# A decoder trunk on one core: another place for the compression MLP's first products in the second layer, and a written-out order for the mixers' preparation buffers

## The chip, the cores and the metric

One core of one Trainium2 chip runs the whole program in one launch. The metric is the device time of one execution in microseconds (us), as the median of several executions.

## What is computed

A decoder of DEPTH = 2 layers on one sequence of S = 256 tokens and D = 1024 channels, all in float32. Cut to what matters here:

```
for l in range(DEPTH):
    h = rms_norm(x, norm1_g[l]);  proj = h @ w_in[l]
    ya = dsa_mixer(...)      # A, number 0: sparse attention with an indexer
    yb = moba_mixer(...)     # B, number 1: block attention
    yc = nsa_mixer(...)      # C, number 2: compressed + selected + window attention
    yd = swa_mixer(...)      # D, number 3: sliding window, 2 kv heads
    x = x + sum_n(sigmoid(gate_n) * (y_n @ w_branch[n])) @ w_out[l]
    x = x + conv_ffn(rms_norm(x, norm2_g[l]))
# inside nsa_mixer, for keys (i = 0) and values (i = 1): 15 blocks of 32 tokens
c_i = gelu((blocks_i + pe_i) @ w1_i) @ w2_i     # w1_i: 2048 x 128
```

The product with `w1_i` is the first product of the compression MLP. It can run as soon as the mixer C has written the blocks with their position encoding, and the mixer C needs it for its compressed keys and values, thus for everything that comes after them.

## The kernel before

**Weights.** All weights are streamed from HBM by SyncE's queue into three buffers `raw` of 1 MB, in the order of a list `plan`, filled by `rows_chunk` and walked by `next(it)`. A chunk of a big matrix holds 4 blocks of 128 rows by 512 columns and is cut in two pieces. Each piece is split in two fp32r parts: ScalarE copies the high part (tile `hi`, `split_hi`), VectorE subtracts it and keeps the rest (tile `lo`, `split_lo`); there are four buffers of each. TensorE then runs `macs`: for each piece 8 matmuls with `hi` (against the activations' high and low parts, `ahi` and `alo`) and 4 with `lo` (against `ahi`). Half a gate (512 of its 1024 columns) is two chunks, so four pieces or 48 matmuls; half a branch's output product is one piece or 12.

**Order of the work.** `Flow` is a planner that runs while the program is built. Streams (Python generators) yield the engine that they want next, the futures that they need and the rings from which they take a buffer; `Flow.run` keeps a model clock for each engine, starts the stream that its clocks let start first, and breaks ties by priority. The instructions of each engine are in the order in which the planner gave them out, and every engine executes its own strictly in that order. The main stream (`main`) goes through the columns of `w_in` for the four mixers, then through a list written out by hand, `SEQ`:

```
SEQ = [("gate", 0, 0), ("gate", 0, 1), ("hidden", 0, 0), ("hidden", 1, 0), ("gate", 1, 0),
       ("gate", 1, 1), ("branch", 0, 0), ("branch", 0, 1), ("gate", 2, 0), ("gate", 2, 1),
       ("branch", 1, 0), ("branch", 1, 1), ("gate", 3, 0), ("branch", 2, 0), ("branch", 2, 1),
       ("branch", 3, 0), ("gate", 3, 1), ("branch", 3, 1)]
```

Both the list of chunks (so the loads on SyncE) and TensorE's work follow it: `gate_of(n, half)`, `hidden(i, ch, hid)`, `branch_out(n, half)`. After it come `w_out`, the convolutional FFN and, in the first layer, the second layer's start.

**The mixers** (`dsa`, `moba`, `nsa`, `swa`) run beside that list: VectorE, ScalarE and GpSimd prepare queries and keys (per-head RMS with a power of -1/2 on GpSimd, rotary), and their transposes (tile `tr`), scores and products with the values stand on TensorE in between the gates' matmuls. All four use one set of preparation buffers `rt`, `qr`, `kr`, `kn` (ring `prep_r`, one entry), so the preparation of one mixer starts only when the one before has given the set back: `(prep,) = yield "ACT", [pf, tab_f[l]], [prep_r]`. Which mixer gets it next is the planner's choice.

**hidden(i, ch, hid)** is the first product of the compression MLP: 16 slices of `w1_i` (raw, not split) against `kr`, which holds C's blocks with the position encoding added (`kr<-kn,col`, the step of `nsa` after which it sets `hid.ready`). TensorE cannot pass it: where `kr` is late, everything behind it waits. The halves' sums `hsum` (`hidden_sum`) lead on to the compressed attention (`nsa_cmp`) and to the two `attend2` streams of C, the last products of which (`tr<-f,slotQ`) close C's output in `slotQ`. `y_T` splits that output for `branch(2,0)` into `yhi` (ScalarE) and `ylo` (VectorE).

A row of the profile calls nearly every instruction L214, the line of the helper in `Eng` that issues it, and L242 for loads; so instructions are told apart by their tiles. Each of the transposes is a matmul that writes `tr`; `mm` and `sc` are the other PSUM banks. Of the two layers, the first has its `hidden` at 101.92 us of the span, the second at 524.06 us.

Of the kernel before, what the change touches and what calls it, by code (L numbers as in the profile page):

```python
# [231 lines left out]
def trunk(ctx: ExitStack, tc: tile.TileContext, a, out):  # L232
# [15 lines left out]
    def ring(n, shape, name, dt=F32):  # L248
# [12 lines left out]
    prep_r = Ring([(sb([128, NT, 512], "rt"), sb([128, NT, 256], "qr"), sb([128, NT, 256], "kr"),  # L261
                    sb([128, NT, 256], "kn"))])
# [73 lines left out]
    col_f = [Fut() for _ in range(DEPTH)]  # L336
    tab_f = [Fut() for _ in range(DEPTH)]
# [46 lines left out]
    def rows_chunk(src, k0, k1, c0, c1):  # L384
# [7 lines left out]
        if not plan:  # L392
# [1 line left out]
        plan.append(Chunk(ap, (nk, n), cut))  # L394


    SEQ = [("gate", 0, 0), ("gate", 0, 1), ("hidden", 0, 0), ("hidden", 1, 0), ("gate", 1, 0),
           ("gate", 1, 1), ("branch", 0, 0), ("branch", 0, 1), ("gate", 2, 0), ("gate", 2, 1),
           ("branch", 1, 0), ("branch", 1, 1), ("gate", 3, 0), ("branch", 2, 0), ("branch", 2, 1),
           ("branch", 3, 0), ("gate", 3, 1), ("branch", 3, 1)]  # L400
    FIRST, LAST = [n for op, n, _ in SEQ if op == "branch"][0], SEQ[-1][1]
    PRIO = (4, 19, 7, 6)
    PORDER = (0, 2, 1, 3)
    CH_A, CH_C = [(0, 384), (384, 680)], [(1448, 1832), (1832, 2100)]
# [4 lines left out]
    for l in range(DEPTH):  # L409
        wi = a["w_in"][l]  # L410
        for kg in range(2):
            for _, c0, c1 in COLS[:2]:
                rows_chunk(wi, 4 * kg, 4 * kg + 4, c0, c1)
        for _, c0, c1 in COLS[2:]:
            for kg in range(2):
                rows_chunk(wi, 4 * kg, 4 * kg + 4, c0, c1)
        for op, n, half in SEQ:
            if op == "gate":
                for kg in range(2):
                    c0 = 2612 + n * D + half * 512  # L420
                    rows_chunk(wi, 4 * kg, 4 * kg + 4, c0, c0 + 512)
            elif op == "hidden":
                ap = a["c_cmp_w1"][l, n].rearrange("(c p) h -> p c h", p=128)
                plan.append(Chunk(ap, (16, 128), []))
            elif n == LAST:
                rows_chunk(a["w_branch"][l, n], 0, 2, half * 512, half * 512 + 512)
            elif half == 0:
                ap = a["w_branch"][l, n].rearrange("(k p) n -> p k n", p=128)
                plan.append(Chunk(ap, (2, D), [lambda v, h=h: v[:, :, h * 512:h * 512 + 512] for h in range(2)]))
        for kg in range(2):  # L430
            for half in range(2):
                rows_chunk(a["w_out"][l], 4 * kg, 4 * kg + 4, half * 512, half * 512 + 512)
        up = a["w_up"][l].rearrange("(k p) (g n) -> p k g n", p=128, g=2)
        for c in range(0, KF, 2):
            for g in range(2):
                plan.append(Chunk(up[:, :, g, c * 128:c * 128 + 256], (8, 256),
                                  [lambda v, h=h: v[:, :, h * 128:h * 128 + 128] for h in range(2)]))
        for half in range(2):
            for k0, k1 in DOWN:
                rows_chunk(a["w_down"][l], k0, k1, half * 512, half * 512 + 512)  # L440
# [358 lines left out]

    def dsa(l, pa, pf, y, yf):  # L800
        m = M[l]
        (prep,) = yield "ACT", [pf, col_f[l]], [prep_r]
        rt, qr, kr, kn = prep
        latT = kn[:, :, 128:256]
        tl = yield from head_rstd(pa[:, :, None, 256:384], 1, 128, sm1["rl"], rt, [])
        tb, = yield "PE", [], [tr_r]
        tp = tb[:, :256].rearrange("p (t q) -> p t q", t=NT)
        for t in range(NT):
            te = P.transpose(tp[:, t, :], pa[:, t, 256:384], ident)
        yield "ACT", [te], []  # L810
        te = A.activation(latT, tp, AF.Copy, scale=m["col"][:, 16:17])
        tr_r.give(tb, te)
        tb, = yield "PE", [te], [tr_r]
        kvp = tb[:, :256].rearrange("p (t q) -> p t q", t=NT)
        for t in range(NT):
            te = P.matmul(kvp[:, t, :], latT[:, t, :], m["kvup"], start=True, stop=True)
        ti = yield from head_rstd(pa[:, :, None, 640:672], 1, 32, sm1["ri"], rt, [])
        yield "DVE", [te, tl], []
        tkv = V.tensor_tensor(kvA, kvp, sm1["rl"][:, :, None].to_broadcast([128, NT, 128]), op=ALU.mult)
        tr_r.give(tb, tkv)  # L820
        yield "DVE", [tab_f[l]], []
        tq = yield from rope(qr.rearrange("p t (h u d) -> p t h u d", u=1, d=32), heads(pa[:, :, 384:640], 32), 8, 32,
                             cosi, sini, rt, [])
        (ix,) = yield "PE", [], [qk_r]
        iqT, ikT = ix[:, 0:512].rearrange("p (k s) -> p k s", k=2), ix[:, 512:768].rearrange("p (k s) -> p k s", k=1)
        tq = yield from T_pairs(iqT, qr, 2, [tq])
        yield "DVE", [ti], []
        ikn = kn[:, :, None, 0:32]
        tn = V.tensor_tensor(ikn, pa[:, :, None, 640:672], sm1["ri"][:, :, None, None].to_broadcast([128, NT, 1, 32]), op=ALU.mult)
        krd = kr[:, :, 0:128]  # L830
        tk = yield from rope(krd.rearrange("p t (h u d) -> p t h u d", h=1, d=32), ikn, 1, 32, ci, si, rt, [tn], dup=4)
        tk = yield from T_pairs(ikT, krd, 1, [tk])
        iw = th(sm1["iw"], 8)
        yield "DVE", [], []
        V.tensor_scalar(iw, pa[:, :, 672:680], 1.0 / 16.0, None, op0=ALU.mult)
        idx_d = []
        idx_f = Fut()
        fin = qk_done(ix, idx_d, idx_f, NT)
        self_f = [Fut() for _ in range(NT)]
        for t in range(NT):  # L840
            fl.spawn(indexer(t, iqT, ikT, iw, [tq, tk], fin, self_f[t]), 5 + t)
        trk = yield from head_rstd(kvA[:, :, None, 0:64], 1, DH, sm1["rk"], rt, [tkv])
        yield "DVE", [trk], []
        knv = kn[:, :, None, 0:64]
        tn = V.tensor_tensor(knv, kvA[:, :, None, 0:64], sm1["rk"][:, :, None, None].to_broadcast([128, NT, 1, 64]), op=ALU.mult)
        tk = yield from rope(krd.rearrange("p t (h u d) -> p t h u d", h=1, d=64), knv, 1, DH, cc[:, 1], ss_[:, 1], rt, [tn], dup=2)
        trq = yield from head_rstd(heads(pa[:, :, 0:256]), H, DH, sm1["rqA"], rt, [])
        yield from scaled(sm1["sA"], sm1["rqA"], H, trq)
        tq = yield from rope(qr.rearrange("p t (h u d) -> p t h u d", u=1, d=64), heads(pa[:, :, 0:256]), H, DH,
                             cc[:, 0], ss_[:, 0], rt, [])  # L850
        (qk,) = yield "PE", [], [qk_r]
        qT, kT = qk[:, 0:512].rearrange("p (k s) -> p k s", k=2), qk[:, 512:768].rearrange("p (k s) -> p k s", k=1)
        tq = yield from T_pairs(qT, qr, 2, [tq])
        tk = yield from T_pairs(kT, krd, 1, [tk])
        prep_r.give(prep, tk)
        fin = qk_done(qk, [], yf, 1)
        fl.spawn(attend2(10, qT, lambda h: 0, kT, lambda h, b: kvA[:, b, 64:128], th(sm1["sA"], H), sel,
                        y, [tq, tk] + self_f, fin=fin), 10)
# [35 lines left out]
        f.t = V.tensor_tensor(sel[t], sel[t], mask, op=ALU.min)  # L894

    def moba(l, pb, pf, y, yf):
        (prep,) = yield "ACT", [pf, tab_f[l]], [prep_r]
        rt, qr, kr, kn = prep
        tr = yield from head_rstd(heads(pb[:, :, 0:512]), 8, DH, sm1["rB"], rt, [])
        yield from scaled(sm1["sB"], sm1["rB"], 8, tr)  # L900
# [13 lines left out]
                        th(sm1["sB"], H), [tri[:, 128:], tri], y, [tq, tk], fin=fin), 20)  # L914

    def swa(l, pd, pf, y, yf):
        (prep,) = yield "ACT", [pf, tab_f[l]], [prep_r]
        rt, qr, kr, kn = prep
        tr = yield from head_rstd(heads(pd[:, :, 0:384]), 6, DH, sm1["rD"], rt, [])
        yield from scaled(sm1["sD"], sm1["rD"], 6, tr)  # L920
# [16 lines left out]

    def nsa(l, pc, pf, y, yf, hid):
        m = M[l]
        (prep,) = yield "DVE", [pf, tab_f[l]], [prep_r]  # L940
        rt, qr, kr, kn = prep
        kvd = kr.rearrange("p t (i u d) -> p t i u d", i=2, u=2)
        t1 = yield from rope(kvd[:, :, 0:1], pc[:, :, None, 256:320], 1, DH, cosd, sind, rt, [], dup=2)
# [322 lines left out]
    def main():  # L1266
# [13 lines left out]
        for l in range(DEPTH):  # L1280
# [11 lines left out]
            proj = (pa, pb, pc, pd)  # L1292
            ys = [p[:, :, 0:256] for p in proj]
            yf = [Fut() for _ in range(4)]
            def mixer(n, f):
                if n == 2:
                    fl.spawn(nsa(l, pc, f, ys[2], yf[2], hid), PRIO[2])
                else:
                    fl.spawn((dsa, moba, None, swa)[n](l, proj[n], f, ys[n], yf[n]), PRIO[n])
# [3 lines left out]
            for i, kg in [(0, 0), (1, 0), (0, 1), (1, 1)] + [(i, kg) for i in range(2, len(COLS)) for kg in range(2)]:  # L1303
                n, c0, c1 = COLS[i]
# [4 lines left out]
                if kg == 1:  # L1309
                    f = Fut()  # L1310
# [54 lines left out]
                        k0 = 4 * half + 2 * j  # L1365
                        fl.spawn(rows_T(mg[:, :, 128 * k0:128 * k0 + 256], [f], mT, k0, mf[2 * half + j], scale=0.5), 2)

            order = [n for op, n, half in SEQ if op == "branch" and half == 0]
            for i, n in enumerate(order):
                yTs[n] = [], Fut()  # L1370
                fl.spawn(y_T(ys[n], yf[n], *yTs[n]), 2)
            for op, n, half in SEQ:
                if op == "gate":
                    yield from gate_of(n, half)
                elif op == "hidden":
                    yield from hidden(n, next(it), hid)
                else:
                    yield from branch_out(n, half)
# [108 lines left out]
```

## Time and profile before

| | |
|---|---|
| median of 3 runs | 851.69 us (851.65 to 853.23) |
| the profiled execution's own time | 850.18 us |
| its span in the trace | 848.4 us |
| mean granted TensorE clock | 0.994 of full speed |
| TensorE busy with matmuls | 835.4 us (98%) |
| VectorE / ScalarE / GpSimd busy | 673.0 (79%) / 543.8 (64%) / 36.5 us (4%) |
| moved by DMA | 149.91 MB, mean 177 GB/s |

Times inside the trace are us from the start of the span. "PE" is TensorE's matmuls, "DVE" VectorE, "ACT" ScalarE, "POOL" GpSimd, "SP" SyncE. Idle time in front of an instruction is given with what released it. The granted clock (PEclk) is a share of full speed: 1.00 is 2.4 GHz, 0.50 is 1.2 GHz, a value in between a stretch with both.

### The profile page before, as it was taken

To read this page: it belongs to the slowest core of one execution; us is meant where nothing else is said; L and a number is where in the kernel's file an instruction comes from. 1 tells how busy PE (TensorE), PEld (TensorE's weight loads), DVE (VectorE), ACT (ScalarE), POOL (GpSimd) and SP (SyncE) were. 2 spreads that over 40 slices of the span, in tenths; PEclk is the share of its full clock that TensorE was granted. 3 is DMA by queue.
4 is the path that set the end of the run, shared out by engine and by line. 5 is a ranking of instruction groups with operands and counts; after the bars stand their busy time and mean duration, and the time that the engine had idled before them with its cause. 6 is when DMAs were issued, how large, how long until landed. Compare 5 with 4: busy or idle time off the path is not lost.

```text
span 848.4 us, 14190 instructions
## 1 busy us (share of the span) xinstructions
PE 835.4 (98%) x5459; PEld 733.1 (86%) x5459; DVE 673.0 (79%) x1327; ACT 543.8 (64%) x941; POOL 36.5 (4%) x33
## 2 busy tenths in 40 slices
PE   9999999999999999999999997999999999999998
PEld 8987787888899999978898875878878999999886
DVE  5799989788579999975458989977676799999552
ACT  6673775765478888844366667766445788888431
POOL 0111111000000000000001110100000000000000
PEclk9999999999999999999999997999999999999999
DMA  7754563444647666546456453435455465665550
GB/s 264 248 199 149 178 216 106 159 162 153 219 138 229 207 201 197 186 153 210 132 168 211 157 173 115 148 117 182 162 192 192 149 199 199 200 199 199 175 197 26
DMA packets 103414, 149.91 MB, mean 177 GB/s; under 512 B 4072, under 2 KB 62258, under 8 KB 103346
## 3 DMA queue, kind: packets, MB, share of 16 engines
q1 hardware_dynamic: 103346, 149.00, 52.6%
q8 instruction: 43, 0.70, 0.3%
q14 instruction: 25, 0.20, 0.1%
HBM read 147.94 MB, written 1.05 MB: 176 GB/s over the span
## 4 chain that ended last, share of the span: by engine, by line
PE 86%; DVE 7%; DMA 2%; POOL 2%; ACT 1%; issue 1%; SPq 0%; DVEq 0%; ACTq 0%
PE mm L214 75%; PE tr L214 6%; PE sc L214 5%; DVE lo L214 2%; DMA raw<-in_w_in_dram 1%; POOL rB L214 1%; DVE acc L214 1%; DVE rt L214 1%; DMA x<-in_x_dram 1%; POOL rD L214 1%; DVE m L214 1%; DVE f L214 1%; ACT f L214 0%; ACT hi L214 0%; SPq L242 0%
## 5 line engine op out<-in xcount | busy, mean ns | idle before, releaser
L214 DVE TENSOR_TENSOR lo<-raw,hi 128x1024 fp32r<-128x1024 f32 (+2 forms) x280 | 328.7, 1179 | 99.4 <-ACT hi L214 95.3
L214 ACT ACTIVATE hi<-raw 128x1024 fp32r<-128x1024 f32 (+2 forms) x280 | 283.0, 1022 | 152.6 <-PE mm L214 132.4
L214 PE MATMUL mm<-hi,ahi 128*128 128x512 f32 (+4 forms) x480 | 176.0, 372 | 0.6 <-ACT hi L214 0.6
L214 PE MATMUL mm<-hi,alo 128*128 128x512 f32 (+4 forms) x480 | 172.2, 364 | 0.0
L214 PE MATMUL mm<-ahi,hi 128*128 128x256 f32 x640 | 149.9, 276 | 0.0
L214 PE MATMUL mm<-alo,hi 128*128 128x256 f32 x640 | 149.7, 276 | 0.0
L214 PEld LDWEIGHTS mm<-alo,hi 128*128 128x128 f32 x640 | 120.1, 188 | 0.1
L214 PEld LDWEIGHTS mm<-ahi,hi 128*128 128x128 f32 x640 | 120.2, 188 | 0.1
L214 PE MATMUL mm<-lo,ahi 128*128 128x512 f32 (+4 forms) x480 | 118.2, 369 | 0.0
L214 PEld LDWEIGHTS mm<-hi,ahi 128*128 128x128 f32 x480 | 90.2, 188 | 15.2 <-issue 1.7
L214 PEld LDWEIGHTS mm<-hi,alo 128*128 128x128 f32 x480 | 90.3, 188 | 12.0
L214 PEld LDWEIGHTS mm<-lo,ahi 128*128 128x128 f32 x480 | 83.0, 188 | 13.2 <-issue 1.3
L214 PE MATMUL mm<-hi,slotQ 128*128 128x512 f32 x352 | 89.6, 395 | 0.0
L214 PE MATMUL mm<-ahi,lo 128*128 128x256 f32 x640 | 86.9, 276 | 0.0
L214 PEld LDWEIGHTS mm<-hi,slotQ 128*128 128x128 f32 x352 | 66.1, 188 | 15.4
L214 PEld LDWEIGHTS mm<-ahi,lo 128*128 128x128 f32 x640 | 79.1, 188 | 0.0
L214 ACT ACTIVATE f<-f,col 128x256 f32<-128x256 f32 x88 | 48.1, 594 | 6.4 <-DVE f L214 6.4
L214 PE MATMUL mm<-lo,slotQ 128*128 128x512 f32 x176 | 48.7, 396 | 0.0
L214 PEld LDWEIGHTS mm<-lo,slotQ 128*128 128x128 f32 x176 | 33.0, 188 | 7.6
L214 ACT ACTIVATE qk<-f,col 128x256 f32<-128x256 f32 x88 | 39.2, 495 | 0.0
L214 ACT ACTIVATE f<-f,nmx 128x128 f32<-128x128 f32 (+1 forms) x80 | 35.3, 444 | 4.7 <-DVE nmx L214 4.7
L214 DVE SCALAR_TENSOR_TENSOR f<-f,col,f 128x254 f32<-128x254 f32 x88 | 38.2, 478 | 0.0
(235 smaller groups left out, 1038.6 us busy)
## 6 DMA issues: line engine op xcount, KB each, us to landing
raw<-in_w_up_dram SPq DMA_DIRECT2D x44, 1024.0 KB, 5.0
raw<-in_w_in_dram SPq DMA_DIRECT2D x40, 1024.0 KB, 4.8
raw<-in_w_down_dram SPq DMA_DIRECT2D x20, 1024.0 KB, 4.9
raw<-in_w_out_dram SPq DMA_DIRECT2D x8, 1024.0 KB, 5.3
raw<-in_w_branch_dram SPq DMA_DIRECT2D x6, 1024.0 KB
raw<-in_w_in_dram SPq DMA_DIRECT2D x7, 768.0 KB
raw<-in_w_in_dram SPq DMA_DIRECT2D x4, 592.0 KB, 3.7
raw<-in_w_in_dram SPq DMA_DIRECT2D x4, 536.0 KB, 5.7
```

The lines of the kernel that those rows point to most:

```text
L214: fn(*a, **k)
```

## The change

Three edits. `SEQ` becomes a list per layer, `SEQS`; the first layer's is the old one, and in the second layer's `("gate", 1, 0)` stands ahead of the two `hidden`, so that 48 matmuls and two loads of 1 MB come before them and not behind. A mixer's request for the preparation buffers also waits for its turn, in a fixed order per layer: A, B, C, D in the first, A, B, D, C in the second. And `nsa` asks for the buffers as a step of ScalarE, not VectorE, as the other three do (that concerns the planner's choice alone; no instruction belongs to the request).

```diff
--- before.py
+++ after.py
@@ -394,11 +394,15 @@
         plan.append(Chunk(ap, (nk, n), cut))
 
 
-    SEQ = [("gate", 0, 0), ("gate", 0, 1), ("hidden", 0, 0), ("hidden", 1, 0), ("gate", 1, 0),
+    SEQS = [[("gate", 0, 0), ("gate", 0, 1), ("hidden", 0, 0), ("hidden", 1, 0), ("gate", 1, 0),
            ("gate", 1, 1), ("branch", 0, 0), ("branch", 0, 1), ("gate", 2, 0), ("gate", 2, 1),
            ("branch", 1, 0), ("branch", 1, 1), ("gate", 3, 0), ("branch", 2, 0), ("branch", 2, 1),
-           ("branch", 3, 0), ("gate", 3, 1), ("branch", 3, 1)]
-    FIRST, LAST = [n for op, n, _ in SEQ if op == "branch"][0], SEQ[-1][1]
+           ("branch", 3, 0), ("gate", 3, 1), ("branch", 3, 1)],
+            [("gate", 0, 0), ("gate", 0, 1), ("gate", 1, 0), ("hidden", 0, 0), ("hidden", 1, 0),
+           ("gate", 1, 1), ("branch", 0, 0), ("branch", 0, 1), ("gate", 2, 0), ("gate", 2, 1),
+           ("branch", 1, 0), ("branch", 1, 1), ("gate", 3, 0), ("branch", 2, 0), ("branch", 2, 1),
+           ("branch", 3, 0), ("gate", 3, 1), ("branch", 3, 1)]]
+    FIRST, LAST = [n for op, n, _ in SEQS[0] if op == "branch"][0], SEQS[0][-1][1]
     PRIO = (4, 19, 7, 6)
     PORDER = (0, 2, 1, 3)
     CH_A, CH_C = [(0, 384), (384, 680)], [(1448, 1832), (1832, 2100)]
@@ -414,7 +418,7 @@
         for _, c0, c1 in COLS[2:]:
             for kg in range(2):
                 rows_chunk(wi, 4 * kg, 4 * kg + 4, c0, c1)
-        for op, n, half in SEQ:
+        for op, n, half in SEQS[l]:
             if op == "gate":
                 for kg in range(2):
                     c0 = 2612 + n * D + half * 512
@@ -799,7 +803,8 @@
 
     def dsa(l, pa, pf, y, yf):
         m = M[l]
-        (prep,) = yield "ACT", [pf, col_f[l]], [prep_r]
+        (prep,) = yield "ACT", [pf[0], pf[1], col_f[l]], [prep_r]
+        pf[2]()
         rt, qr, kr, kn = prep
         latT = kn[:, :, 128:256]
         tl = yield from head_rstd(pa[:, :, None, 256:384], 1, 128, sm1["rl"], rt, [])
@@ -894,7 +899,8 @@
         f.t = V.tensor_tensor(sel[t], sel[t], mask, op=ALU.min)
 
     def moba(l, pb, pf, y, yf):
-        (prep,) = yield "ACT", [pf, tab_f[l]], [prep_r]
+        (prep,) = yield "ACT", [pf[0], pf[1], tab_f[l]], [prep_r]
+        pf[2]()
         rt, qr, kr, kn = prep
         tr = yield from head_rstd(heads(pb[:, :, 0:512]), 8, DH, sm1["rB"], rt, [])
         yield from scaled(sm1["sB"], sm1["rB"], 8, tr)
@@ -914,7 +920,8 @@
                         th(sm1["sB"], H), [tri[:, 128:], tri], y, [tq, tk], fin=fin), 20)
 
     def swa(l, pd, pf, y, yf):
-        (prep,) = yield "ACT", [pf, tab_f[l]], [prep_r]
+        (prep,) = yield "ACT", [pf[0], pf[1], tab_f[l]], [prep_r]
+        pf[2]()
         rt, qr, kr, kn = prep
         tr = yield from head_rstd(heads(pd[:, :, 0:384]), 6, DH, sm1["rD"], rt, [])
         yield from scaled(sm1["sD"], sm1["rD"], 6, tr)
@@ -937,7 +944,8 @@
 
     def nsa(l, pc, pf, y, yf, hid):
         m = M[l]
-        (prep,) = yield "DVE", [pf, tab_f[l]], [prep_r]
+        (prep,) = yield "ACT", [pf[0], pf[1], tab_f[l]], [prep_r]
+        pf[2]()
         rt, qr, kr, kn = prep
         kvd = kr.rearrange("p t (i u d) -> p t i u d", i=2, u=2)
         t1 = yield from rope(kvd[:, :, 0:1], pc[:, :, None, 256:320], 1, DH, cosd, sind, rt, [], dup=2)
@@ -1292,7 +1300,17 @@
             proj = (pa, pb, pc, pd)
             ys = [p[:, :, 0:256] for p in proj]
             yf = [Fut() for _ in range(4)]
+            order_of = ((0, 1, 2, 3), (0, 1, 3, 2))[l]
+            turn = dict((n, Fut()) for n in order_of)
+            turn[order_of[0]].t = 0.0
+
+            def next_turn(n):
+                i = order_of.index(n) + 1
+                if i < 4:
+                    turn[order_of[i]].t = 0.0
+
             def mixer(n, f):
+                f = [f, turn[n], lambda: next_turn(n)]
                 if n == 2:
                     fl.spawn(nsa(l, pc, f, ys[2], yf[2], hid), PRIO[2])
                 else:
@@ -1365,11 +1383,11 @@
                         k0 = 4 * half + 2 * j
                         fl.spawn(rows_T(mg[:, :, 128 * k0:128 * k0 + 256], [f], mT, k0, mf[2 * half + j], scale=0.5), 2)
 
-            order = [n for op, n, half in SEQ if op == "branch" and half == 0]
+            order = [n for op, n, half in SEQS[l] if op == "branch" and half == 0]
             for i, n in enumerate(order):
                 yTs[n] = [], Fut()
                 fl.spawn(y_T(ys[n], yf[n], *yTs[n]), 2)
-            for op, n, half in SEQ:
+            for op, n, half in SEQS[l]:
                 if op == "gate":
                     yield from gate_of(n, half)
                 elif op == "hidden":
```

The GpSimd steps of the preparation show the order of the mixers: B, C, D in the first layer (`rB`, `rC`, `rD`) and B, D, C in the second (`rB`, `rD`, `rC`), before and after the change alike. In the first layer TensorE's instructions stand in the same order as before. In the second they part behind the last matmuls of `gate(0,1)`.

**TensorE, second layer, from the last matmul of `gate(0,1)`.** Before (`raw_73,kr` and `raw_71,kr` are the two `hidden`, `hi_76` the first piece of `gate(1,0)`):

```order
L214 MATMUL mm_64<-lo_79,ahi 128x512
L214 MATMUL tr_70<-cst,kr 128x128 x4
L214 MATMUL tr_69<-cst,kr 128x128 x4
L214 MATMUL tr_70<-cst,f_0_82 128x128 x4
L214 MATMUL mm_65<-raw_73,kr 15x128 x16
L214 MATMUL mm_66<-raw_71,kr 15x128 x16
L214 MATMUL tr_69<-cst,f_1_83 128x128 x4
L214 MATMUL tr_70<-cst,f_1_83 128x128 x4
L214 MATMUL mm_63<-hi_76,ahi 128x512
```

The change, from the end of the second piece of `gate(1,0)` (`lo_81`) into its third (`hi_74`):

```order
L214 MATMUL mm_65<-lo_81,ahi 128x512
L214 MATMUL mm_66<-lo_81,ahi 128x512
L214 MATMUL mm_65<-hi_74,ahi 128x512
L214 MATMUL mm_65<-hi_74,alo 128x512
L214 MATMUL mm_66<-hi_74,ahi 128x512
L214 MATMUL mm_66<-hi_74,alo 128x512
L214 MATMUL tr_69<-cst,kr 128x128 x4
L214 MATMUL tr_70<-cst,f_0_82 128x128 x4
L214 MATMUL mm_65<-hi_74,ahi 128x512
```

and from its last matmul:

```order
L214 MATMUL mm_66<-lo_79,ahi 128x512
L214 MATMUL mm_63<-raw_72,kr 15x128 x16
L214 MATMUL tr_70<-cst,f_1_83 128x128 x4
L214 MATMUL tr_69<-cst,f_1_83 128x128 x4
L214 MATMUL mm_64<-raw_73,kr 15x128 x16
L214 MATMUL tr_70<-cst,hsum 128x15
L214 MATMUL tr_69<-f_3_85,slotQ 64x128 x4
L214 MATMUL tr_69<-f_2_84,slotQ 64x128 x8
```

The `hidden` products, which stood ahead of all of `gate(1,0)`, are now behind its 48 matmuls. The transposes of `kr`, which stood ahead of it too, are now within it: the first group (D's keys) four matmuls into the second piece, the second group (C's blocks), which is shown, four matmuls into the third.

**TensorE, second layer, the last products of C with its values** (`f_2_84`, `f_3_85` with `slotQ`). Before, with the first matmuls of the piece that follows:

```order
L214 MATMUL tr_69<-f_2_84,slotQ 64x128 x4
L214 MATMUL tr_69<-f_3_85,slotQ 64x128 x8
L214 MATMUL mm_65<-hi_76,ahi 128x512
L214 MATMUL mm_65<-hi_76,alo 128x512
L214 MATMUL mm_66<-hi_76,ahi 128x512
L214 MATMUL mm_66<-hi_76,alo 128x512
```

The change:

```order
L214 MATMUL tr_69<-f_2_84,slotQ 64x128 x4
L214 MATMUL tr_69<-f_3_85,slotQ 64x128 x8
L214 MATMUL mm_65<-lo_79,ahi 128x512
L214 MATMUL mm_66<-lo_79,ahi 128x512
L214 MATMUL mm_65<-lo_79,ahi 128x512
L214 MATMUL mm_66<-lo_79,ahi 128x512
L214 MATMUL mm_63<-hi_76,yhi_114 128x512
L214 MATMUL mm_63<-hi_76,ylo_115 128x512
L214 MATMUL mm_64<-hi_76,yhi_114 128x512
L214 MATMUL mm_64<-hi_76,ylo_115 128x512
```

Before, they stood in `gate(2,1)`, and 96 more matmuls of gates and branches came between them and `branch(2,0)`, whose first is `sc_68<-hi_76,yhi_114`; now they stand within `gate(3,0)`, four matmuls with `lo_79` ahead of `branch(2,0)`, whose first is `mm_63<-hi_76,yhi_114`.

**VectorE, second layer, at D's norm** (`rD` from the sum of squares to the scale `sD`; the power of -1/2 on GpSimd stands between `rD<-rD` and `sD<-rD`). Before:

```order
L214 COPY qk_88<-tr_69 128x512
L214 TENSOR_TENSOR lo_79<-raw_72,hi_75 128x1024
L214 TENSOR_REDUCE rD<-rt 128x12
L214 RECIPROCAL rd_113<-den_111 128x4
L214 TENSOR_SCALAR rD<-rD 128x12
L214 TENSOR_SCALAR f_1_83<-f_1_83,rd_113 128x256 x2
L214 TENSOR_SCALAR sD<-rD 128x8
```

The change:

```order
L214 COPY qk_88<-tr_69 128x512
L214 TENSOR_TENSOR lo_79<-raw_72,hi_75 128x1024
L214 RECIPROCAL rd_113<-den_111 128x4
L214 TENSOR_TENSOR lo_80<-raw_73,hi_76 128x1024
L214 TENSOR_REDUCE rD<-rt 128x12
L214 TENSOR_SCALAR f_1_83<-f_1_83,rd_113 128x256
L214 TENSOR_SCALAR rD<-rD 128x12
L214 TENSOR_TENSOR lo_81<-raw_73,hi_77 128x1024
L214 COPY f_2_84<-tr_69 128x512
L214 TENSOR_TENSOR lo_78<-raw_71,hi_74 128x1024
L214 TENSOR_SCALAR sD<-rD 128x8
```

Between the reduction and `sD` VectorE now has two splits (`lo_81`, `lo_78`) and a copy, where before it had two scalings; one split (`lo_80`) also stands ahead of the reduction.

On SyncE, the two chunks of `gate(1,0)` are now loaded ahead of the two of `w1`, the other way round than before.

## Rows read from the trace of the kernel before

**Rows 1.** Windows by stage: us, busy of PE, PEld, DVE, ACT, POOL, PEclk, DMA.

```profile
440.00:515.23 75.23, 75.03 (x462) 63.72 (x460) 67.23 (x181) 47.55 (x83) 11.06 (x6) 1.00 0.53 175
515.23:528.39 13.16, 7.36 (x84) 5.66 (x85) 11.89 (x42) 9.82 (x29) 1.64 (x1) 0.61 0.32 108
528.39:614.75 86.36, 86.36 (x503) 69.65 (x502) 67.11 (x184) 51.95 (x112) 2.21 (x2) 1.00 0.45 156
```

**Rows 2.** Waits of PE in the whole span: total us, times, longest.

```profile
PE tr L214 <- DVE kr L214: 3.0, 1, 3.0
PE tr L214 <- DVE den L214: 1.8, 1, 1.8
PE mm L214 <- DVE kr L214: 1.0, 1, 1.0
...
PE sc L214 <- DVE slotP L214: 0.2, 1, 0.2
```

**Rows 3.** Chain of waits in 514 to 530: start us, us, what.

```profile
517.45 0.62 DVE kr L214 x3
...
520.46 0.49 DVE kr L214 x2
```

**Rows 4.** Windows of the idle and the half-speed pieces of 515.23 to 528.39.

```profile
515.23:518.21 2.98, 0.00 (x1) 0.03 (x1) 2.98 (x13) 1.07 (x2) 0.00 (x0) 0.83 0.69 226
518.21:519.31 1.10, 1.08 (x4) 0.68 (x4) 0.66 (x5) 0.53 (x3) 0.00 (x0) 0.50 0.90 349
519.31:521.10 1.79, 0.00 (x0) 0.03 (x1) 1.70 (x7) 1.79 (x10) 0.00 (x0) 0.50 0.00 0
521.10:523.04 1.94, 1.94 (x8) 1.54 (x8) 1.43 (x5) 1.89 (x8) 0.00 (x0) 0.50 0.00 0
...
524.06:527.61 3.55, 3.55 (x65) 2.59 (x66) 3.39 (x13) 3.40 (x7) 1.64 (x1) 0.53 0.13 31
```

**Rows 5.** Windows at full clock: the first layer's hidden, and eight transposes.

```profile
101.92:103.79 1.87, 1.87 (x65) 1.66 (x64) 1.86 (x11) 1.47 (x4) 0.00 (x0) 1.00 0.78 300
507.79:508.58 0.79, 0.79 (x9) 0.79 (x8) 0.00 (x0) 0.15 (x1) 0.79 (x1) 1.00 1.03 399
```

**Rows 6.** DVE in order of time: start us, us, what [idle before].

```profile
504.39 1.23 DVE L214 TENSOR_TENSOR lo<-raw,hi 128x1024 fp32r<-128x1024 f32 x1
505.53 0.95 DVE L214 TENSOR_REDUCE rD<-rt 128x12 f32<-128x768 f32 x1
...
509.11 0.17 DVE L214 TENSOR_SCALAR sD<-rD 128x8 f32<-128x8 f32 x1 [1.90 <-POOL rD L214]
...
511.73 1.22 DVE L214 TENSOR_TENSOR lo<-raw,hi 128x1024 fp32r<-128x1024 f32 x1
...
523.65 1.16 DVE L214 TENSOR_TENSOR kr<-kn,col 128x120 f32<-128x120 f32 x4
```

**Rows 7.** POOL, the power step of D (first and second layer), and DVE beside it.

```profile
131.03 1.22 DVE L214 TENSOR_TENSOR lo<-raw,hi 128x1024 fp32r<-128x1024 f32 x1
...
131.20 3.17 POOL L214 TENSOR_TENSOR rD<-rD,mhalf 128x12 f32<-128x12 f32 x1 [9.22 <-DVE rD L214]
...
506.77 2.31 POOL L214 TENSOR_TENSOR rD<-rD,mhalf 128x12 f32<-128x12 f32 x1 [18.28 <-DVE rD L214]
```

**Rows 8.** PE, DVE and ACT in order of time, from C's last products to branch(2,0).

```profile
592.80 0.68 DVE L214 TENSOR_TENSOR slotQ<-slotQ,tr 128x512 f32<-128x512 f32 x1
...
603.78 0.64 ACT L214 ACTIVATE yhi<-slotQ 128x512 fp32r<-128x512 f32 x1 [2.65 <-DVE mg L214]
...
604.45 0.69 DVE L214 TENSOR_TENSOR ylo<-slotQ,yhi 128x512 fp32r<-128x512 f32 x1
...
613.65 1.08 PE L214 MATMUL mm<-lo,ahi 128*128 128x512 f32 x4
614.57 0.39 PE L214 MATMUL sc<-hi,yhi 128*128 128x512 f32 x1
```

**Rows 9.** DMA issues (page, part 6): count, KB each, us to landing.

```profile
raw<-in_w_in_dram SPq DMA_DIRECT2D x40, 1024.0 KB, 4.8
```

## The prediction

> **What bounds the kernel.** TensorE is busy 98% of the span, so the time is its matmuls plus what it waits or runs slowly. I read four views in turn. The waits of PE [rows 2] are short but for three, 3.0, 1.8 and 1.0 us, all for VectorE. The windows by stage [rows 1] put them together: from 515.23 to 528.39 PE is busy 7.36 of 13.16 us at a mean clock of 0.61, whereas it is busy 75.03 of 75.23 us in the stage before and all of the 86.36 us behind, at 1.00. The chain of waits [rows 3] says who is late: VectorE's steps to `kr`, for D's keys (ready 517.45 + 0.62 = 518.07), then C's blocks (520.95), then the blocks with their encoding, which `hidden` needs. The pieces of that stretch [rows 4] show the second half of the loss: after 2.98 us without a matmul the clock is at half, and stays there nearly to the end of `hidden`.
>
> **What the change can give back.** Three idle pieces: 2.98, 1.79 and 524.06 - 523.04 = 1.02, together 5.79 us [rows 4]. The work between them runs at half speed, and its price at full speed stands elsewhere [rows 5]: eight transposes take 0.79 us, so four 0.40, and the first layer's `hidden` takes 1.87 us. So 1.10 - 0.40 = 0.70, 1.94 - 0.79 = 1.15 and 3.55 - 1.87 = 1.68, together 3.53 us. In all **9.32 us**, if TensorE now has 48 matmuls of `gate(1,0)` to do while VectorE finishes `kr`, and if `kr` is not late again.
>
> **Is kr in time?** Four matmuls of 128x512 take 614.57 - 613.65 = 0.92 us [rows 8], a piece of twelve 2.75 us. From 515.23 PE comes to D's transposes at 515.23 + 2.75 + 0.92 = 518.9, to C's at 515.23 + 5.5 + 0.92 + 0.4 = 522.05, and to `hidden` at 515.23 + 11.0 + 1.2 for the twelve transposes = 527.4. VectorE's side is replayed from rows 6 in the changed order; operations overlap by some 0.08 us, so a split counts 505.53 - 504.39 = 1.14 us. At 505.53 come a reciprocal (0.1), the split now ahead (1.14), the reduction (0.87), a scaling (0.3) and `rD` (0.1): 508.05. Then GpSimd's power: 2.31 us in the second layer, where VectorE idled until `sD`, 3.17 us in the first, where a split ran beside it, so 0.86 more for a split [rows 6, 7]. Now two splits and a copy stand beside it (1.14 + 0.6 + 1.14 = 2.9, until 510.95). So `sD` comes between 511.0 (no slowing) and 513.3 (the power only after both splits, 510.95 + 2.31); by the nearest row, two splits at 0.86, at 508.05 + 0.1 + 2.31 + 1.72 = 512.2, which I take. Before it came at 509.11.
>
> From `sD` to D's `kr` there were 518.07 - 509.11 = 8.96 us, in which stood two splits, the one at 511.73 and another [rows 6]. Both now stand elsewhere: 8.96 - 2.28 = 6.7, so 518.9 and 0.1 of hand-over, 0.1 behind PE. C's `kr` took 2.9 us more; one split (1.14) and a scaling (0.2) now stand among that, and 0.46 us of waiting for slow transposes falls away: 522.7, some 0.5 behind a PE that is itself 0.1 late. `hidden`'s `kr` took from `sD` 523.65 + 1.16 - 509.11 = 15.7 us; less two splits, plus one, 14.55: 526.75, **0.7 us ahead of PE** at 527.4, 1.3 with the waits before it. So of the three waits some 0.6 us is left.
>
> A rule of the Trainium skill speaks against this step. "SBUF — State Buffer", section "SBUF: two separate sides", makes the port pair that VectorE and GpSimd share an exclusive lock: a VectorE operation with two SBUF inputs, or a GpSimd one, holds it for the whole instruction and the other fully blocks. By the Trainium skill the copy would let the power in and the second split would wait for it, or the power would wait for both, which puts `sD` up to 1.1 us later than my sum. The 3.17 against 2.31 us agrees with a lock; that VectorE is held up in turn no row here shows. By the rule's worst order the time would be that of rival 1, 845.3.
>
> **What the change adds.** C's compressed attention begins 3.3 us later (527.4 for 524.06), and TensorE reaches everything behind sooner. The order shows what is late next: C's last products with its values now stand four matmuls ahead of `branch(2,0)`. Before, `slotQ` was finished at 593.48 and `branch(2,0)` began at 614.57, 21 us later [rows 8], so no wait there is seen. Now the closing addition (0.61), `yhi` (0.62) and `ylo` (0.60), durations of rows 8, stand between, and three hand-overs of about 0.05; 2.0 us, less the 0.92 of the four matmuls: a **wait of 1.0 us**. Bounds: 0, if TensorE is late itself and covers it; 2.1, if a split of 1.14 stands in VectorE's way. I take 1.0 as the sum of the rows.
>
> Other waits: the 0.6 us above, bounds 0 (`sD` at 511.0) and 1.7 (513.3). VectorE was busy 67.23 + 11.89 + 67.11 = 146.2 of 174.75 us from 440 to 614.75 [rows 1]; without 9.3 us it is busy 88%, and `gate(3,0)` now writes the PSUM banks that `branch(1,0)` left 12 matmuls (2.75 us) earlier, with four operations of VectorE of some 0.6 us between. For that I take one wait like the nearest row, 0.2 us [rows 2], bounds 0 and 1. Together **0.8**.
>
> At nothing I cost: the exchange of loads (a chunk lands 4.8 us after its issue [rows 9]; the chunk of `gate(1,0)` now takes the buffer that `w1` had, over 10 us before it is needed, and `w1` comes while `gate(1,0)` runs; if this cover went, `hidden` would wait up to 4.8 us); the written-out turns, as GpSimd's order of B, C, D and B, D, C shows that the planner had chosen the same; and the request on ScalarE, which has no instruction. The first layer's order on TensorE is unchanged. Below zero, a gain besides the 9.32 us, I exclude: elsewhere PE has no idle time beyond 0.2 us in 161 us [rows 1].
>
> **Sum**, against the profiled execution: 850.18 - 9.32 + 1.0 + 0.8 = 842.66 us. The median stands 851.69 - 850.18 = 1.51 higher, so **844.2 us**. The bounds of the added terms come to 0 and 2.1 + 1.7 + 1.0 = 4.8, so this case lies between 842.4 and 847.2.
>
> **Rivals.**
> 1. *`kr` late again.* The power waits for both splits, `sD` comes at 513.3: 1.1 us more of waits at the transposes, too short to bring the clock down: 845.3. For it: 3.17 beside one split. Against: even so the chain meets 48 matmuls, 11 us, where it was 5.8 us late. 0.10.
> 2. *The half speed is no part of the gain.* The three runs lie 1.5 us above the profiled one, so something differs between executions; if the clock did not fall in them, only 5.79 - 1.8 = 3.99 us is gained: 847.7. Against: 2.98 us without a matmul brought it down here [rows 4]. 0.10.
> 3. *A new wait brings the clock down again.* If the wait at `branch(2,0)` or one on C's chain grows to 2 or 2.5 us in one piece, it may bring back the half speed, as 2.98 us did [rows 4], with 3.53 us as bound: 850.18 - 9.32 + 2.25 + 3.53 + 0.8 + 1.51 = 849.0. For it: VectorE at 88%. 0.12.
> 4. *Slower.* C's output gets so late that PE stands at `branch(2,0)` for w and then runs slowly: w + 3.53 + 0.8 outweighs 9.32 from w = 5.0 us on. With w = 8 it is 850.18 - 9.32 + 8 + 3.53 + 0.8 + 1.51 = 854.7. C's chain took 593.48 - 524.06 = 69.4 us; PE comes to `branch(2,0)` at 614.57 - 9.32 + 0.8 = 606.0, so from `hidden` at 528 the chain to `slotQ` would have to take 606.0 + 5.0 - 1.2 - 528 = 82 us. Against: it would have to stretch by 18%. 0.04.
> 5. *No visible change*: the gain is lost in many small waits of VectorE, over 6 us in all: 851. 0.03.
>
> **Numbers.** The forecast has 0.61. A measurement can tell some 0.2%, 1.7 us, from no change: 850.0 to 853.4 is "same". Faster: 0.61 + 0.10 + 0.10 + 0.10 = 0.91, the last being most of rival 3; same: its rest and rival 5, 0.05; slower 0.04. The range goes from 842.0 (hardly a new wait, and the 0.4 us by which the median may sit lower) to 849.0, rival 3's centre; it leaves out rivals 4, 5 and half of 3, some 0.13.
>
> **What would show it.** Right: in the changed profile no wait of PE for `kr` over 1 us, the clock at 1.00 through 515 to 530, `hidden` at 527.4 to 528.5 and 1.9 us long, GpSimd's `rD` at 3 to 4 us, a wait of about 1 us at the first `yhi` or `ylo` of `branch(2,0)`, and the first layer as before. Wrong: over 2 us of wait on C's chain between 530 and 610 with a clock of 0.50 behind it (rivals 3 and 4), `hidden` still behind VectorE (1), or all of this as forecast and the time above 847 (2).

## The result, and the profile after

The changed kernel takes 842.05 us (median of 4 runs, 841.77 to 842.51), the one before 851.67 us beside it: a ratio of 0.989, with a 95% interval from 0.9866 to 0.9914. The forecast was 844.2 us in a range from 842.0 to 849.0, with 0.91 for faster; the median lies at the lower end of that range, 0.05 us inside it. The profiled execution took 841.77 us, its span fell from 848.4 to 839.9 us, TensorE's busy time from 835.4 to 832.3 us, and the mean granted clock rose from 0.994 to 1.0.

The windows of the changed kernel, with the same columns as [rows 1]; the last row is the stage of C's remaining attention up to `branch(2,0)`, which begins at 605.92 and not at 614.57 us:

```profile
440.00:515.23 75.23, 75.03 (x463) 63.95 (x462) 68.89 (x183) 47.95 (x84) 11.93 (x6) 1.00 0.56 189
515.23:528.39 13.16, 13.16 (x92) 10.62 (x91) 12.10 (x38) 11.60 (x32) 2.44 (x1) 1.00 0.24 82
528.39:606.00 77.61, 77.26 (x496) 62.04 (x492) 64.75 (x182) 49.25 (x112) 2.39 (x3) 1.00 0.50 177
```

The stretch that cost the kernel before 5.8 us of idle time and a clock of 0.61 is now full and at 1.00. PE's waits in the whole span show no `kr` and no `den` any more (3.0, 1.0 and 1.8 us, [rows 2]), and two new ones at `branch(2,0)`:

```profile
PE mm L214 <- ACT yhi L214: 0.3, 1, 0.3
...
PE mm L214 <- DVE ylo L214: 0.2, 1, 0.2
```

The chain that was replayed by hand ahead of the run, engine by engine in order of time: VectorE around GpSimd's power (to set beside [rows 6]), the power itself (beside [rows 7]), then PE where it needs each `kr`:

```profile
507.75 1.22 DVE L214 TENSOR_TENSOR lo<-raw,hi 128x1024 fp32r<-128x1024 f32 x1
...
509.49 1.21 DVE L214 TENSOR_TENSOR lo<-raw,hi 128x1024 fp32r<-128x1024 f32 x1
511.12 0.17 DVE L214 TENSOR_SCALAR sD<-rD 128x8 f32<-128x8 f32 x1 [0.43 <-POOL rD L214]
...
516.99 0.89 DVE L214 TENSOR_TENSOR kr<-rt 128x128 f32<-128x128 f32 x4
...
520.97 0.48 DVE L214 TENSOR_TENSOR kr<-rt 128x128 f32<-128x128 f32 x2
...
523.89 1.19 DVE L214 TENSOR_TENSOR kr<-kn,col 128x120 f32<-128x120 f32 x4
```

```profile
507.92 3.17 POOL L214 TENSOR_TENSOR rD<-rD,mhalf 128x12 f32<-128x12 f32 x1 [19.60 <-DVE rD L214]
525.95 2.63 POOL L214 TENSOR_TENSOR rC<-rC,mhalf 128x8 f32<-128x8 f32 x1 [14.86 <-DVE rd L214]
```

```profile
518.63 0.60 PE L214 MATMUL tr<-cst,kr 128*128 128x128 f32 x4
...
521.83 0.60 PE L214 MATMUL tr<-cst,kr 128*128 128x128 f32 x4
...
527.39 1.07 PE L214 MATMUL mm<-raw,kr 128*15 128x128 f32 x32
```

`kr` is ready at 517.88, 521.45 and 525.08, PE comes to it at 518.63, 521.83 and 527.39: 0.8, 0.4 and 2.3 us in hand. The new wait is at `branch(2,0)`, on PE and VectorE (to set beside [rows 8]):

```profile
602.94 1.53 PE L214 MATMUL tr<-f,slotQ 128*64 128x128 f32 x24
604.40 1.20 PE L214 MATMUL mm<-lo,ahi 128*128 128x512 f32 x4
605.92 0.49 PE L214 MATMUL mm<-hi,yhi 128*128 128x512 f32 x1 [0.32 <-ACT yhi L214]
606.64 0.50 PE L214 MATMUL mm<-hi,ylo 128*128 128x512 f32 x1 [0.23 <-DVE ylo L214]
```

```profile
604.51 0.69 DVE L214 TENSOR_TENSOR slotQ<-slotQ,tr 128x512 f32<-128x512 f32 x1 [1.78 <-PE tr L214]
605.90 0.69 DVE L214 TENSOR_TENSOR ylo<-slotQ,yhi 128x512 fp32r<-128x512 f32 x1 [0.70 <-ACT yhi L214]
```

The four `lo` matmuls are issued by 605.3, and a stream of `yhi` and `ylo` matmuls starts one every 0.23 us. The first starts at 605.92 and the second at 606.64, not 605.3 and 605.5: 606.64 - 605.53 = 1.1 us lost, though the waits list counts only 0.3 and 0.2, the time in which by the profile no matmul ran at all.

### The profile page after: what moved, and what is told of

Read it like the earlier page. It is cut to its first block, busy times and chain, and to the rows that moved or that the text cites. A ratio compares the mean times of both kernels' runs of the same rounds, so it can differ in the third digit from the quotient of the medians.

```text
span 839.9 us, 14190 instructions
## 1 busy us (share of the span) xinstructions
PE 832.3 (99%) x5459; PEld 730.8 (87%) x5459; DVE 673.4 (80%) x1323; ACT 543.6 (65%) x945; POOL 37.4 (4%) x33
## 4 chain that ended last, share of the span: by engine, by line
PE 86%; DVE 7%; DMA 2%; POOL 2%; ACT 1%; issue 1%; SPq 0%; DVEq 0%; ACTq 0%
PE mm L214 75%; PE tr L214 6%; PE sc L214 4%; DVE lo L214 2%; DVE acc L214 1%; DMA raw<-in_w_in_dram 1%; POOL rB L214 1%; DVE m L214 1%; DVE rt L214 1%; DMA x<-in_x_dram 1%; ACT hi L214 0%; SPq L242 0%; POOL rD L214 0%; ACT f L214 0%; DVE f L214 0%
```

## The experiments

My theory: the gain is the move of `gate(1,0)` alone; it consists of idle time and half speed; 48 matmuls are enough; and C's output is late next. The times are medians; the kernel before, beside them, took 850.95 (e1 to e4), 851.25 (e5 to e8) and 851.17 us (e9 to e11).

**Which edit?** e1 keeps the turns and the request, with the old list in both layers; e2 moves `gate(1,0)` alone.

```diff
# e1: second layer's list
-("gate", 0, 1), ("gate", 1, 0), ("hidden", 0, 0), ("hidden", 1, 0),
+("gate", 0, 1), ("hidden", 0, 0), ("hidden", 1, 0), ("gate", 1, 0),
# e2: nsa, and no turns in main
-(prep,) = yield "ACT", [pf[0], pf[1], tab_f[l]], [prep_r]
+(prep,) = yield "DVE", [pf, tab_f[l]], [prep_r]
```

> Edit: the turns and the request on ScalarE are kept, the second layer's list is the old one (hidden ahead of gate(1,0)). Theory (the whole gain is the move of gate(1,0)): TensorE's order is that of before, only three small VectorE rows of the first layer are swapped, so the time stays at that of before, 851.7 within 1.7 us, with waits of PE for kr of 3.0, 1.8 and 1.0 us and the clock at 0.50 about 518 to 527. Rival (the written-out order of the preparation buffers brings the gain): 842 to 844 and no wait for kr.

> Edit: gate(1,0) ahead of the two hidden in the second layer, without turns and with nsa's request on VectorE as before. Theory: the same time as the change, 842.05 within 0.5 us, hidden at 527.4, no wait for kr, a wait of about 1.1 us at branch(2,0). Rival (turns needed): slower than the change by several us, with C's preparation in another place.

e1 took 850.74 us (ratio 0.9995, 0.9985 to 1.0004), and its three waits stand as before:

```profile
PE tr L214 <- DVE kr L214: 3.3, 1, 3.3
PE tr L214 <- DVE den L214: 1.8, 1, 1.8
...
PE mm L214 <- DVE kr L214: 1.0, 1, 1.0
```

e2 took 841.68 us (0.9891, 0.9874 to 0.9908) with the change's waits at `branch(2,0)`. From the second layer's power step `rB` to the end of the span there are 363.71 us before, 364.56 in e1, 355.39 in the change and 355.43 in e2. So the move is the whole gain, and for this list no worth of the turns shows. This mark has a scatter of its own where the clock falls: e1 and the kernel before differ by 0.85 us behind it. TensorE's order from `hidden` on is the same in both; the first wait is 0.3 us longer in e1, and the eight transposes behind `hidden` take 1.70 us there and 1.09 us before.

**How much of it was the half speed?** e3 is the kernel before with filling: while PE would wait for `kr`, it transposes the identity into a free bank.

```diff
+def fill(hid):
+    bank, = yield "PE", [], [mm_r]
+    while hid.go is None:
...
+        t = P.transpose(bank[:, :128], ident, ident)
```

> Edit: the kernel before, with 49 transposes of the identity (each some 0.10 us at full clock, 21 + 16 + 1 + 11 of them) as filling in front of D's kr transposes, C's kr transposes, the scaled scores and hidden of the second layer; they compute nothing that is used. Theory (the loss was 5.79 us of idle time and 3.53 us of half speed, which are two things): the clock stays at 1.00, the 3.53 us come back but the idle time stays (filled, not used): 850.18 - 3.53 = 846.7 for the profiled execution, up to 848.5 if some filling is in the way of kr, and the runs spread less than the 4 us of the kernel before. Rival (the half speed lay in VectorE's shadow and cost nothing): 850 to 852. Second rival (the clock falls all the same, by idle time between the fillings): 851 and more.

It took 849.06 us: 0.9976 (0.9966 to 0.9985), 1.9 us less than before, not the 3.5 us on which my 846.7 rested. PE of e3 in order of time, and the windows of that stretch:

```profile
514.14 2.45 PE L214 MATMUL mm<-cst 128*128 128x128 f32 x21
517.64 0.63 PE L214 MATMUL tr<-cst,kr 128*128 128x128 f32 x4 [1.05 <-DVE kr L214]
518.11 1.91 PE L214 MATMUL mm<-cst 128*128 128x128 f32 x16
...
523.11 1.94 PE L214 MATMUL mm<-raw,kr 128*15 128x128 f32 x64
```

```profile
514.96:528.00 13.04, 11.39 (x141) 9.64 (x141) 12.22 (x44) 9.65 (x29) 1.67 (x1) 1.00 0.46 144
```

The clock stays at 1.00 and `hidden` takes 1.94 in place of 3.55 us, so 1.6 us came back there. But `hidden` starts 39.36 us after the second layer's `rB` step (at 483.75), and before it started 524.06 - 484.69 = 39.37 us after it. The transposes were faster and `hidden` not sooner: what they lost at half speed, 0.70 + 1.15 us, lay beside VectorE's chain. From `rB` to the end e3 has 362.72 us, 1.0 less than the profile before and 1.8 less than e1's; its TensorE order behind `hidden` is not quite that of before, and it has a new wait of 0.3 us for `hsum`. So the half speed was worth 1 to 2 us, not 3.5. The runs spread over 2.0 us (848.06 to 850.03), which does not tell them from the others of this study.

**Is it the lateness of C's `kr`?** e4 removes the same wait another way: the old list, but C prepared ahead of D in the second layer too.

```diff
-order_of = ((0, 1, 2, 3), (0, 1, 3, 2))[l]
+order_of = ((0, 1, 2, 3), (0, 1, 2, 3))[l]
```

> Edit: the old list in both layers, but the preparation buffers go A, B, C, D in the second layer too, so C's kr is prepared ahead of D's. Theory (hidden waited because C's kr stood behind all of D's preparation on VectorE): hidden starts right behind gate(0,1) at about 515.2 without a wait and takes 1.9 us, the clock stays up; 9.3 us fewer than before and no wait at branch(2,0), as C's chain begins 12 us sooner: 841 to 842.5, as fast as the change or 1 us faster. Rival (D is then late: its keys come 20 us later): a wait of over 2 us for D's output or in between, 843 to 848.

```profile
515.47 1.94 PE L214 MATMUL mm<-raw,kr 128*15 128x128 f32 x64 [0.45 <-DVE mx L214]
```

842.92 us (0.9904, 0.9889 to 0.9919). `hidden` starts at 515.47, 31.0 us after `rB` and not 39.4, at full clock; the 0.45 us in front of it are put down to another operation of VectorE (`mx`), not to `kr`. In place of the old waits there are two for VectorE's merges (`slotP`), 1.3 us. That is 0.4 us above my range, and not for D's output. So two different edits that make `kr` come in time bring most of the same gain: 8.0 us here and 9.3 us in e2, against the same runs of the kernel before.

**How far can `hidden` be moved?** e5 puts both halves of the gate ahead.

```diff
-("gate", 1, 0), ("hidden", 0, 0), ("hidden", 1, 0), ("gate", 1, 1),
+("gate", 1, 0), ("gate", 1, 1), ("hidden", 0, 0), ("hidden", 1, 0),
```

> Edit: the change, but with both halves, gate(1,0) and gate(1,1), ahead of the two hidden in the second layer, 96 matmuls instead of 48. Theory (48 matmuls are enough for kr, and C's output is the next thing late): hidden at about 539 without a wait, nothing more gained, and PE waits at C's last products or at branch(2,0) for 4 to 10 us, with the half speed behind it if it is one wait of over 2 us: 846 to 855, so slower than the change by 4 us or more. Rival (C's chain has slack and can be squeezed by 11 us): 842 to 843.5.

853.07 us, slower than the kernel before (1.0027, 1.0014 to 1.0039) and 11 us slower than the change. PE of e5, and the window around it:

```profile
606.63 1.09 PE L214 MATMUL tr<-cst,f 128*128 128x128 f32 x4 [3.88 <-DVE f L214]
609.17 1.97 PE L214 MATMUL tr<-cst,f 128*128 128x128 f32 x8 [1.45 <-ACT f L214]
615.42 0.50 PE L214 MATMUL mm<-hi,yhi 128*128 128x512 f32 x1 [1.52 <-ACT yhi L214]
```

```profile
585.00:625.00 40.00, 32.91 (x179) 26.22 (x178) 28.76 (x76) 20.52 (x52) 0.20 (x1) 0.87 0.22 69
```

This is the mechanism of my fourth rival, at 96 matmuls: C's output is late. The first and longest wait is at the transposes of C's last softmax, 3.9 us, ahead of `branch(2,0)`, which waits another 1.5 us; the clock falls (0.87 over these 40 us, eight transposes take 1.97 us), and more is lost than `hidden` ever cost. `hidden` itself starts at 543.62 us, without a wait, and not at 539 as I had expected: more of the mixers' products came to stand ahead of it. With 48 matmuls only `branch(2,0)` is late, by 1.1 us.

**Is the rest at `branch(2,0)`?** e6 lets C's branch change places with D's in the second layer (`LAST` becomes one per layer); e10 and e11 repeat the change and e6 side by side.

```diff
-("gate", 2, 0), ("gate", 2, 1), ... ("gate", 3, 0), ("branch", 2, 0), ("branch", 2, 1),
-("branch", 3, 0), ("gate", 3, 1), ("branch", 3, 1)
+("gate", 3, 0), ("gate", 3, 1), ... ("gate", 2, 0), ("branch", 3, 0), ("branch", 3, 1),
+("branch", 2, 0), ("gate", 2, 1), ("branch", 2, 1)
```

> Edit: the change, and in the second layer C's branch changes places with D's: gates 0, 1, 3, 2 and branches 0, 1, 3, 2, so branch(2,0) comes 24 matmuls later and D's branch, whose output is long there, stands in front of it. Theory (the wait of 1.1 us at branch(2,0) is all that the change left in this stage): it goes, 842.05 - 1.1 = 841.0 within 0.4 us. Rival (the wait is covered by something else late, or comes back at w_out): 842 within 0.4 us.

> The change itself once more, as the yardstick for the next kernel on the same chip: 842.0 within 0.5 us.

> e6 once more, beside the change on the same chip: 840.9 within 0.5 us, so 1.1 us below the change. Rival (the 1.1 us between them were chance): within 0.4 us of the change.

e6 took 840.96 us (0.9876, 0.9861 to 0.9891), e11 841.33 (0.9885, 0.987 to 0.99), e10 841.68 (0.9892, 0.9877 to 0.9907). PE of e6 passes into D's branch without a gap:

```profile
604.23 1.21 PE L214 MATMUL mm<-lo,ahi 128*128 128x512 f32 x4
605.28 0.40 PE L214 MATMUL mm<-hi,yhi 128*128 128x512 f32 x1
605.51 0.40 PE L214 MATMUL mm<-hi,ylo 128*128 128x512 f32 x1
```

From the second layer's `rB` to the end e6 has 354.29 and e11 354.30 us, the change 355.39 and e10 355.42: the 1.1 us are there each time. Of the whole time the pair e10 and e11 alone shows 0.35 us, inside the bound that I had set for chance; over the eight runs of each the medians are 841.93 for the change (841.2 to 842.76) and 841.09 for e6 (840.42 to 841.87). So e6 has the lowest median of this study. The 1.1 us behind the mark are shown; that the whole program is faster is not shown by the one pair taken side by side, and the 0.8 us between the eight runs rest on runs taken at different times. In both of its traces `rB` also comes 0.5 us later than in those of the change, with the same orders up to there; why stays open.

**Does the first layer take it too?** e7 moves `gate(1,0)` there as well, e8 joins the change with e4's order, e9 is e7 with D ahead of C in the first layer.

```diff
# e7: first layer's list as the second's
# e8: -order_of = ((0, 1, 2, 3), (0, 1, 3, 2))[l]
#     +order_of = ((0, 1, 2, 3), (0, 1, 2, 3))[l]
# e9: e7, and
#     +order_of = ((0, 1, 3, 2), (0, 1, 3, 2))[l]
```

> Edit: the change, and gate(1,0) ahead of the two hidden in the first layer too. Theory (in the first layer kr was ready 6 us ahead of hidden, so there is nothing to gain there): 842.05 within 0.8 us. Rival (the place of hidden has a worth of its own, by its loads or by VectorE's load): over 1.5 us faster or slower.

> Edit: both ways at once in the second layer, the preparation in the order A, B, C, D and gate(1,0) ahead of the two hidden. Theory (each way removes the same wait, so they don't add): the same as the better of the two alone, 841 to 842.5. Rival (they add, or the place of hidden itself matters): under 839.

> Edit: e7 (gate(1,0) ahead of the two hidden in both layers) with the order A, B, D, C of the preparation buffers in the first layer too. Theory (e7 lost 20 us because C holds the buffers until after hidden and the steps behind it, so D's preparation came 20 us later; it is the order of the buffers that lets hidden be moved at no cost): D's power step in the first layer comes ahead of C's, no wait for D's output, 842 to 845. Rival (the first layer has no room for a later hidden, whoever goes first): over 855.

e7: 862.65 us, e8: 848.73 us, both far from my theory, which had looked at `kr` alone. The clue is GpSimd's steps of the first layer, in e7 and then in the change:

```profile
98.74 2.54 POOL L214 TENSOR_TENSOR rC<-rC,mhalf 128x8 f32<-128x8 f32 x1 [22.32 <-DVE rC L214]
132.94 0.54 POOL L214 TENSOR_TENSOR crs<-crs,mhalf 15x1 f32<-15x1 f32 x1 [31.66 <-DVE crs L214]
139.29 2.55 POOL L214 TENSOR_TENSOR rkC<-rkC,mhalf 128x8 f32<-128x8 f32 x1 [5.81 <-DVE rkC L214]
150.94 2.27 POOL L214 TENSOR_TENSOR rD<-rD,mhalf 128x12 f32<-128x12 f32 x1 [9.10 <-DVE rD L214]
```

```profile
97.90 2.54 POOL L214 TENSOR_TENSOR rC<-rC,mhalf 128x8 f32<-128x8 f32 x1 [21.77 <-DVE rC L214]
119.12 0.54 POOL L214 TENSOR_TENSOR crs<-crs,mhalf 15x1 f32<-15x1 f32 x1 [18.68 <-DVE cg L214]
...
131.03 3.17 POOL L214 TENSOR_TENSOR rD<-rD,mhalf 128x12 f32<-128x12 f32 x1 [9.24 <-DVE rD L214]
```

C takes the preparation buffers before `hidden` and gives them back only after its last keys, which the program has behind the compressed ones (`crs`). With `hidden` at 117.34 us, not 101.7, `crs` comes 13.8 and D's `rD` 19.9 us later. C's and D's softmax are then late (PE waits up to 4.7 us for D's, and from 185 to 225 us the clock is at 0.79), and the first layer is 20.6 us longer (`rB` to `rB`: 432.81, in the change 412.19). e8 shows the same in the second layer: `rD` at 559.88 us, where e4 has it at 548.07, and 2.3 and 1.4 us of waits for `yhi`. e9 puts the theory to the test: D goes first in the first layer, with `hidden` as late as in e7. Its GpSimd steps:

```profile
95.24 2.27 POOL L214 TENSOR_TENSOR rD<-rD,mhalf 128x12 f32<-128x12 f32 x1 [17.09 <-DVE rD L214]
113.69 1.64 POOL L214 TENSOR_TENSOR rC<-rC,mhalf 128x8 f32<-128x8 f32 x1 [16.18 <-DVE rd L214]
```

843.2 us (0.9906, 0.9889 to 0.9922): 19 us of e7's loss are gone by the order of the buffers alone. It is 1.5 us slower than the change beside it (e10), so the first layer has nothing to gain here. So the list and that order belong together: `hidden` may be late only where nobody waits for the buffers that C holds.

## Why the prediction was right, and where its sizes were off

- **The three waits go, 5.79 us.** Right: e1 and e2, and no `kr` in the waits after.
- **Half speed, 3.53 us.** Right in the sum, as the whole stretch is full and at 1.00 after; as a cost of its own it was over-sized. removed by itself it gives back 1.9 us by the medians (e3): the slow transposes lay beside VectorE's work. The 9.32 us are one loss with one cause, VectorE's lateness.
- **Rival 2, the clock not falling in the other runs.** The record answers it: the granted clock is 0.992 to 0.996 in all 39 runs of the kernel before that stand beside the experiments, 0.999 to 1.0 in those of the change (e10). And e2 is 7.4 us faster than e3, in which the clock stays up and the chain of VectorE is as late as before; the rival left 3.99.
- **`kr` in time.** The mechanism was right and one term mis-sized: "two splits at 0.86, at 508.05 + 0.1 + 2.31 + 1.72 = 512.2, which I take". The power took 3.17 us beside two splits as beside one, so one of the two terms of 0.86 had no counterpart; `sD` came at 511.12, 1.1 us sooner, and of the 0.6 us of waits at the transposes nothing was left. That this is near my lower bound of 511.0 is chance: the bound stood for a power that is not slowed, and this one was slowed once. The 0.2 us for PSUM banks did not come either.
- **`branch(2,0)`, 1.0 us.** 1.1 us measured, at the place and for the operands that were named; e6 removes it. This term was right in mechanism and size.
- **The sum.** For the profiled execution -9.32 + 1.8 = -7.5 was forecast. From the second layer's `rB` on the traces give 355.39 - 363.71 = -8.3, which is -9.32 + 1.1 within 0.1: the 0.8 us of other waits (0.6 at the transposes, 0.2 for PSUM banks) were not there. The agreement within 0.1 is in part luck, since with e1's profile in place of before's it would be -9.2.
- **The median's 1.51 us.** This makes up 1.2 of the 2.1 us between 844.2 and 842.05: I carried the distance of three runs from one profile over to the new kernel, where it is 0.28 us (842.05 - 841.77). It was chance on both sides: the medians of before in the three later comparisons are 850.95, 851.25 and 851.17 us, so the three runs lay some 0.6 us high and the one profiled execution some 0.9 us low. The median of all 39 runs is 851.1, and 841.93 over the eight of the change: a gain of 9.2 us, nearer to the 9.32 than to my 7.5. That the forecast's range still held the result, by 0.05 us, is luck.
- **Turns and request at nothing.** Right for this list (e1, e2); e7 and e8 show that the order is not worth nothing as such.
- **Rival 4, slower.** Its mechanism is that of e5, reached with 48 more matmuls; the longest wait stands earlier on C's chain than the rival had it.

## What to carry to other kernels

Where an engine that executes in order waits for a product that is late, put work that is ready ahead of it, and then ask two things: what now comes late at the end of the chain (here 1.1 us, at twice the move 11 us), and which shared buffers the moved step's owner holds meanwhile (here 20 us, where another mixer queues for them). Don't count the half speed behind a wait as a gain that could be had by itself: keeping the clock up brought 1 to 2 of its 3.53 us, the rest came only with the late engine off the path. Compare executions from a mark in the stage to the end, not by the whole span, when the beginning varies by more than the question, and take more than one profile of each kernel: behind the mark three profiles of the change's order agree within 0.05 us, two of the old order differ by 0.85.

## What the runs showed of the hardware that was not expected

- A power on GpSimd was longer where a VectorE split was already running when it started, and not where a split began while it was under way. D's (128x12) took 2.31 us with no split beside it and 3.17 with one that had begun 0.17 us earlier (both in [rows 7]); it took 3.17 again in the change, where a second split began 1.57 us into it (507.92). In e9 it took 2.27 us though two splits began within it, at 95.67 and 96.80 us. C's (128x8) took 2.63 us with a split running at its start and another behind it (525.95), and 1.64 where the first split began 0.5 to 0.6 us into it (e4, e8 and e9). The splits took their 1.21 to 1.23 us in each of these cases. The Trainium skill, "SBUF — State Buffer", section "SBUF: two separate sides", has the one of the two engines that starts first hold the shared ports for its whole instruction while the other fully blocks. The trace agrees where the split began first, and not where the power did: the splits then ran at their full pace. So the power does not seem to hold the ports while it computes. That reading was not tried by itself.
- Executions of one kernel differ by 1 to 5.1 us, and part of that lies at the beginning. Up to the first layer's `rB` all kernels of this study have the same orders, and in their thirteen profiles it starts between 71.50 and 74.35 us (the latest is e9's, whose profiled execution took 846.17 us against a median of 843.2). The profiles of the change, e2 and e10 have spans of 838.97 to 839.90 us; `rB` in the first layer starts at 71.56 to 72.32, and from the second layer's `rB` to the end they agree within 0.05 us. Where the clock falls there is another part: the 0.85 us between the kernel before and e1.
